# A two-layer hybrid encoder in float32: seven- and eight-product pairs alternate, weight sums one pair ahead, banks emptied by token tile, side loads on GpSimd's queue

## The chip, the core and the metric

The kernel runs on one core of a Trainium2 chip. Its engines are TensorE (PE, the matmuls; its weight loads are listed as PEld), VectorE (DVE), ScalarE (ACT), GpSimd (POOL) and SyncE (SP), which here does nothing but issue loads and stores. The metric is the device time of one execution in microseconds (us), the median of several runs.

## What is computed

An encoder with two layers over 256 tokens of width 2048, in float32. Each layer adds to x a mixer and then a feed-forward network (FFN):

```
h = rms_norm(x, g_mix[l])
z = h @ w_in[l]                          # one projection for mixer and memory queries
tok = chunked_spatial_gating(...)        # layer 0: gelu, 128-token chunks, 12 groups
tok = gqa_axial_attention(...)           # layer 1: 12 query heads, 4 key heads, QK norm, rotary
mem_out = memory_attention(q_mem, mem)   # both: 4 heads over 256 memory tokens
x = x + concat(tok, mem_out) @ w_out[l]
gate, up = split(rms_norm(x, g_ffn[l]) @ w_gate_up[l])   # 2048 -> 2 x 5632
x = x + (silu(gate) * up) @ w_down[l]                    # 5632 -> 2048
```

## The kernel before

**Tiles.** Tokens lie in two tiles (t = 0, 1) of 128. Weights are read in column blocks of 512 and rows (K blocks) of 128. Every product of float32 numbers is made of three matmuls of reduced operands, high x high, low x high and high x low (`matmul3`, L195 to L197). A weight tile `raw` is cut by `halves`: ACT casts it to `whi` (L248), DVE subtracts to get `wlo` (L249). Activations are cut in the same way by `split` (L189, L190). Transposes are matmuls against `ident` (L201 for most, L473 for the softmax weights).

**Linear layers.** `Linear` runs a column block for both token tiles: load of four K blocks (L262), `halves`, 24 matmuls. All projections use it, w_down too.

**Gate and up.** `Pair` works one column block f of 512 gate and 512 up columns (11 of them) over 16 K blocks, two at a time: eight feature pairs i. A pair of two K blocks, two token tiles and two column blocks is a 2 x 2 product of blocks. `eight` does it with eight `matmul3`. `seven` does it with seven, in Winograd's form of Strassen's scheme: it needs sums of weights (`T`, L342 to L344, on DVE, and a second `halves` of T) and sums of activations (`activation_sums`, once for each layer and pair). The seven products land in banks 1 to 7 of the accumulators, eight's in banks 2, 3, 4 and 8. Banks 1, 5, 6, 7 come from a pool of four with the tag `m`, which transposes and scores use too; 2, 3, 4, 8 from a pool of four with the tag `acc`. When the sevens are through, `inner` adds banks 1, 5, 6, 7 into four tiles `e` (L372 to L376); when the last pair is through, `outer` adds banks 2, 3, 4, 8 to these (L381 to L385). Silu and the product follow, and later the transposes of the result (`turn_a`).

**Which pairs.** Pairs 0, 1, 2 are sevens. In block f = 0 of a layer the order is 3, 4, 5, 6, 7, 0, 1, 2 (the activation sums are not ready at first), in all others 0, 1, 2, 3, ..., 7. Blocks f = 0 to 3, 4 to 7 and 8 to 10 are each followed by the part of the down-projection that uses them, which `Linear` runs over four column blocks, and DVE adds the result to X.

**Order.** The program is written stage by stage. Work that is to stand further back is put there by `later(delay, fn)`, which counts ticks; a tick is called after a group of products (half a pair, or half a unit of `Linear`). From the order written so, a scheduler makes a fixed row of instructions for each engine; each engine works through its row in order and waits for semaphores.

**Queues and buffers.** SP's queue issues every weight load, the loads of the memory tokens (L524), their transposed copies to DRAM for layer 1 (`memT`, L535) and back, and `w_spatial` (L590); ACT's queue issues `g_v` (L592) and the small constants. `raw`, `whi` and `wlo` have three buffers each, `T` two. A load waits on its queue until its buffer is free, and what is behind it on that queue waits too.

**Memory.** `Memory.prep` loads eight pieces of the memory tokens, one for each tick in layer 0 and one for every second in layer 1, and two ticks later transposes each.

**Attention.** `attend` gives each block of four query heads: transposes of q, scores (128x256 matmuls), reduce (L454), exponentials on ACT (L458), reciprocal, scaling (L463), transposes (L473), weighting. The ticks at which its parts run are a tuple of four delays.

Of the kernel before, what the change touches and what calls it, by code (L numbers as in the profile page):

```python
# [16 lines left out]
P = 128  # L17
D = 2048
S = 256
DEPTH = 2  # L20
# [31 lines left out]
def encoder(ctx: ExitStack, tc: tile.TileContext, x, mem, g_mix, g_ffn, w_in_a, g_v_a, w_spatial, b_spatial,  # L52
# [191 lines left out]
    def halves(raw, n):  # L244

        hi = wp.tile([P, KC4, NB], F32R, tag="whi", name=nm("whi"))[:, :n]
        lo = wp.tile([P, KC4, NB], F32R, tag="wlo", name=nm("wlo"))[:, :n]
        nc.scalar.copy(hi, raw)  # L248
        nc.vector.tensor_tensor(lo, raw, hi.bitcast(F32), ALU.subtract)  # L249
        return [(hi[:, c, :], lo[:, c, :]) for c in range(n)]  # L250

    class Linear:
# [12 lines left out]
        def run(self, units):  # L265
            for k0, n in units:
# [3 lines left out]
                parts = halves(raw[:, :n], n)  # L270
# [23 lines left out]
    def activation_sums(a):  # L294

        res = []
        for c in (0, 2):
            q = big(F32, [P, 4, P])
            nc.vector.tensor_tensor(q[:, 0], a[1][:, c], a[1][:, c + 1], ALU.subtract)
            nc.vector.tensor_tensor(q[:, 2], a[1][:, c], a[0][:, c], ALU.subtract)  # L300
            nc.vector.tensor_tensor(q[:, 1], a[0][:, c], q[:, 0], ALU.subtract)
            nc.vector.tensor_tensor(q[:, 3], a[0][:, c + 1], q[:, 1], ALU.subtract)
            hi, lo = split(q, [P, 4, P])
            res.append([(hi[:, i, :], lo[:, i, :]) for i in range(4)])
        return res

    class Pair:
# [3 lines left out]
        def __init__(self, parts, sums, w, na, nb, order, fast):  # L311
            self.parts, self.sums, self.w, self.na, self.nb = parts, sums, w, na, nb
            self.order, self.fast, self.bank, self.part = order, fast, {}, {}
            last = [i for i in order if i in fast][-1]
            rest = [i for i in order if i not in fast]
            for i in order:
                raw = self.fetch(i)
                (self.seven if i in fast else self.eight)(i, raw)
                if i == last:
                    self.inner()  # L320
            self.outer(bool(rest))
# [8 lines left out]
        def add(self, name, a, b, i):  # L330
# [3 lines left out]
            some = len([x for x in self.order if x in self.fast])  # L334
            many = len(self.order) - some
            of = {1: some, 5: some, 6: some, 7: some, 8: 2 * many}.get(name, some + 2 * many)
            self.part[name] += 1
            matmul3(self.bank[name], a, b, self.part[name] == 1, self.part[name] == of)

        def seven(self, i, raw):  # L340
            T = room["p"].tile([P, KC4, NB], F32, tag="T", name=nm("T"), bufs=2)
            nc.vector.tensor_tensor(T[:, 0:2], raw[:, 1:4:2], raw[:, 0:1].to_broadcast([P, 2, NB]), ALU.add)  # L342
            nc.vector.tensor_tensor(T[:, 2], T[:, 0], raw[:, 3], ALU.add)  # L343
            nc.vector.tensor_tensor(T[:, 3], T[:, 2], raw[:, 2], ALU.add)  # L344
# [8 lines left out]
            for some in (inner, outer):  # L353
                for name, a, b in some:
                    self.add(name, a, b, i)
                tick()

        def eight(self, i, raw):
            w01, w00, w10, w11 = halves(raw, 4)
            get, k0, k1 = self.parts.get, 2 * i, 2 * i + 1  # L360
            for t, names in ((0, (2, 3)), (1, (4, 8))):
                for name, pair in zip(names, ((w00, w10), (w01, w11))):
                    self.add(name, get(k0, t), pair[0], i)
                    self.add(name, get(k1, t), pair[1], i)
                tick()

        def inner(self):

            b = self.bank
            tmp = [room["p"].tile([P, NB], F32, tag=f"e{i}", name=nm("e"), bufs=1) for i in range(4)]  # L370
            e, v, f, y = tmp
# [5 lines left out]
            self.tmp = tmp  # L377

        def outer(self, rest):
            b, (e, v, f, y) = self.bank, self.tmp  # L380
            nc.vector.tensor_tensor(e, b[2], e, ALU.add)  # L381
            nc.vector.tensor_tensor(v, b[4], v, ALU.subtract)
            nc.vector.tensor_tensor(f, b[3], f, ALU.add)
            if rest:
                nc.vector.tensor_tensor(y, b[8], y, ALU.add)  # L385
            self.out = [[e, f], [v, y]]
# [127 lines left out]
    class Memory:  # L514
# [5 lines left out]
        def prep(self, delay, apart):  # L520
            def load(j, t):
                m = big()
                src = memT[t][j] if self.l else mem[0, t * P:(t + 1) * P, j * NB:(j + 1) * NB]
                nc.sync.dma_start(m, src)  # L524
                later(2, lambda: piece(m, j, t))

            def piece(m, j, t):
# [7 lines left out]
                nc.sync.dma_start(memT[t][j], raw)  # L535
# [23 lines left out]
    def add_residual(acc, j, norm, g, parts):  # L559
# [7 lines left out]
        for t in range(NT):  # L567
            nc.vector.tensor_tensor(X[t][j], acc[t], X[t][j], ALU.add)
            later(1 + t, lambda t=t: turn(t))

# [3 lines left out]
    for l in range(DEPTH):  # L574
# [4 lines left out]
        if l == 0:  # L579
# [28 lines left out]
            def gate(t, c):  # L608
# [4 lines left out]
                sb[t][c] = big()  # L613
# [40 lines left out]
            m.prep(1, 1)  # L654
# [24 lines left out]
        else:  # L679
# [11 lines left out]
            for c in range(3):  # L691
                acc = linear(hT, w, c * NB)
                attend(head_norm(acc, norm.r, ghead["q"], True), (7, 8, 10, 12), lambda: own["k"], lambda: own["v"],
# [15 lines left out]
        fast = [0, 1, 2]  # L709
        slow = [3, 4, 5, 6, 7]  # L710
        sums = {}

        def feature_sums(j):
            whole = []
            for t in range(NT):
                hi, lo = hF.whole[j, t]
                a = big(F32, [P, 4, P])
# [83 lines left out]
```

## Time and profile before

| | |
|---|---|
| three runs | 2088.92, 2092.15, 2092.33 us, median 2092.15 |
| the profiled execution | 2092.77 us |
| its span | 2090.8 us |
| mean granted TensorE clock | 0.991 |
| DMA packets, bytes | 204,696, 396.0 MB, mean 189 GB/s |

The span runs from the first to the last instruction in the trace; the remaining 2 us of the profiled execution lie around it. Times in the trace are counted from the start of the span. In the views of the profile, a row of a group or of a timeline names the line, the engine, the operation and the tiles, output <- inputs; in square brackets stands how long the engine had been idle before it and what ended that. A row of the windows gives for each engine the busy time and, in brackets, the number of instructions; then the share of full clock that TensorE was granted, the DMA engines' busy share and GB/s.

### The profile page before, as it was taken

The numbers are of one execution on the slowest core, as the hardware profiler recorded it, in microseconds if no ns is written. First come the engines' busy times: TensorE is split into PE (matmuls) and PEld (weight loads), VectorE is DVE, ScalarE is ACT, GpSimd is POOL, SyncE is SP. The second block draws the span as 40 slices with busy tenths as digits, with TensorE's granted clock in tenths as the row PEclk, the third lists the DMA queues.
The fourth block names the chain that finished last, engine by engine and source line by source line (L and its number), as shares of the span: only waits on it lengthen the run. The fifth ranks groups of instructions, "written<-read, shape, count | busy, mean of one in ns | idle before, by whom it ended". The sixth has DMA issues, their size and how long they took to land.

```text
span 2090.8 us, 23855 instructions
## 1 busy us (share of the span) xinstructions
PE 2052.3 (98%) x9346; PEld 1697.9 (81%) x9346; DVE 1485.8 (71%) x1502; ACT 1038.9 (50%) x1150; POOL 39.3 (2%) x50
## 2 busy tenths in 40 slices
PE   8799999899999999999999999998999999999999
PEld 6688888688888888888888878877888888888887
DVE  5466557987578875787567776688965889657964
ACT  7555444545344543445555654544543456434542
POOL 0010000000000000000000010000000000000000
PEclk9899999999999999999999999999999999999999
DMA  8655555465556555656556534545565655656564
GB/s 274 233 173 165 187 181 181 162 201 199 184 192 210 201 194 189 201 191 204 186 171 224 172 121 161 182 161 181 181 213 190 202 181 194 210 200 201 178 211 135
DMA packets 204696, 396.01 MB, mean 189 GB/s; under 512 B 9660, under 2 KB 12840, under 8 KB 204584
## 3 DMA queue, kind: packets, MB, share of 16 engines
q1 hardware_dynamic: 202432, 392.86, 56.2%
q10 hardware_dynamic: 2152, 1.63, 0.3%
q8 instruction: 73, 1.20, 0.2%
q14 instruction: 39, 0.32, 0.0%
HBM read 390.26 MB, written 4.19 MB: 189 GB/s over the span
## 4 chain that ended last, share of the span: by engine, by line
PE 92%; DVE 3%; issue 2%; DMA 2%; ACT 1%; SPq 0%; ACTq 0%; DVEq 0%
PE acc L195 27%; PE acc L196 27%; PE acc L197 27%; PE m L195 3%; PE m L196 3%; PE m L197 3%; PE m L201 2%; DVE wlo L249 1%; DMA a<-in_mem 1%; ACT whi L248 1%; PE m L473 0%; DVE T L342 0%; DMA gh_mq<-in_g_mq 0%; PE m L612 0%; DVE T L343 0%
## 5 line engine op out<-in xcount | busy, mean ns | idle before, releaser
L249 DVE TENSOR_TENSOR wlo<-raw,whi 128x2048 fp32r<-128x2048 f32 (+3 forms) x369 | 797.2, 2165 | 368.9 <-ACT whi L248 367.4
L248 ACT CAST whi<-raw 128x2048 fp32r<-128x2048 f32 (+3 forms) x369 | 666.5, 1812 | 646.0 <-PE acc L196 559.6
L195 PE MATMUL acc<-whi,h 128*128 128x512 f32 x1428 | 561.2, 394 | 10.1 <-DVE e L381 8.3
L196 PE MATMUL acc<-whi,h 128*128 128x512 f32 x1428 | 559.0, 392 | 0.0
L197 PE MATMUL acc<-wlo,h 128*128 128x512 f32 x1428 | 540.9, 392 | 0.0
L195 PE MATMUL acc<-whi,a 128*128 128x512 f32 x1154 | 451.5, 392 | 0.6 <-DVE a L404 0.6
L197 PE MATMUL acc<-wlo,a 128*128 128x512 f32 x1154 | 449.7, 391 | 0.0
L196 PE MATMUL acc<-whi,a 128*128 128x512 f32 x1154 | 449.5, 391 | 0.0
L195 PEld LDWEIGHTS acc<-whi,h 128*128 128x128 f32 x1428 | 270.0, 189 | 65.6 <-DVE e L381 9.1
L196 PEld LDWEIGHTS acc<-whi,h 128*128 128x128 f32 x1428 | 269.9, 189 | 55.2
L197 PEld LDWEIGHTS acc<-wlo,h 128*128 128x128 f32 x1428 | 268.7, 188 | 55.5 <-DVE wlo L249 0.4
L197 PEld LDWEIGHTS acc<-wlo,a 128*128 128x128 f32 x1154 | 217.1, 188 | 44.8
L195 PEld LDWEIGHTS acc<-whi,a 128*128 128x128 f32 x1154 | 217.2, 188 | 44.4 <-DVE a L404 0.8
L196 PEld LDWEIGHTS acc<-whi,a 128*128 128x128 f32 x1154 | 217.1, 188 | 44.0
L248 ACT CAST whi<-T 128x2048 fp32r<-128x2048 f32 x66 | 126.2, 1913 | 118.3 <-PE acc L196 110.6
L249 DVE TENSOR_TENSOR wlo<-T,whi 128x2048 fp32r<-128x2048 f32 x66 | 150.9, 2287 | 29.6 <-ACT whi L248 29.6
L342 DVE TENSOR_TENSOR T<-raw 128x1024 f32<-128x1024 f32 x66 | 80.4, 1218 | 18.7 <-DMA raw<-in_w_gate_up 18.7
L195 PE MATMUL m<-whi,a 128*128 128x512 f32 x198 | 80.0, 404 | 1.8 <-ACT whi L248 1.8
L196 PE MATMUL m<-whi,a 128*128 128x512 f32 x198 | 79.4, 401 | 0.0
L189 ACT CAST a<-m 128x512 fp32r<-128x512 f32 x80 | 46.3, 585 | 41.2 <-PE m L197 17.9
L190 DVE TENSOR_TENSOR a<-m,a 128x512 fp32r<-128x512 f32 x80 | 54.1, 684 | 17.0 <-ACT a L189 17.0
L197 PE MATMUL m<-wlo,a 128*128 128x512 f32 x198 | 55.9, 391 | 1.3 <-DVE wlo L249 1.3
(123 smaller groups left out, 1262.3 us busy)
## 6 DMA issues: line engine op xcount, KB each, us to landing
raw<-in_w_gate_up SPq DMA_DIRECT2D x352, 512.0 KB, 4.6
raw<-in_w_down SPq DMA_DIRECT2D x88, 1024.0 KB, 5.1
raw<-in_w_out SPq DMA_DIRECT2D x32, 1024.0 KB, 5.1
raw<-in_w_in_a SPq DMA_DIRECT2D x24, 1024.0 KB, 5.1
raw<-in_w_in_b SPq DMA_DIRECT2D x24, 1024.0 KB, 5.2
raw<-in_w_mem_kv SPq DMA_DIRECT2D x16, 1024.0 KB, 5.2
raw<-in_w_in_a SPq DMA_DIRECT2D x7, 512.0 KB, 5.8
x<-in_x SPq DMA_DIRECT2D x8, 256.0 KB, 4.7
```

What stands on the lines that cost most here:

```text
L189: nc.scalar.copy(hi, src)
L190: nc.vector.tensor_tensor(lo, src, hi.bitcast(F32), ALU.subtract)
L195: nc.tensor.matmul(out, lhsT=a[0], rhs=b[0], start=start, stop=False)
L196: nc.tensor.matmul(out, lhsT=a[1], rhs=b[0], start=False, stop=False)
L197: nc.tensor.matmul(out, lhsT=a[0], rhs=b[1], start=False, stop=stop)
L201: nc.tensor.transpose(dst[:, c * P:(c + 1) * P], src[:, c * P:(c + 1) * P], ident)
L248: nc.scalar.copy(hi, raw)
L249: nc.vector.tensor_tensor(lo, raw, hi.bitcast(F32), ALU.subtract)
L342: nc.vector.tensor_tensor(T[:, 0:2], raw[:, 1:4:2], raw[:, 0:1].to_broadcast([P, 2, NB]), ALU.add)
```

## The change

- **Order of the pairs.** In f > 0: 0, 3, 1, 4, 2, 5, 6, 7. In f = 0: 3, 4, 5, 0, 6, 1, 7, 2, with only pairs 0 and 1 as sevens. The activation sums of pairs 0, 1, 2 are made one at a time, at ticks 2, 4, 6.
- **One pair ahead.** `run` loads the next pair and makes its T before it works on the present one, also across the border of two blocks f (`follow`).
- **Banks.** `outer(t)` adds token tile t's two banks right behind that tile's products of the last pair.
- **Down-projection.** It uses `Pair` too, on two column blocks at a time, and adds straight into X. In the first two of the three groups of blocks one pair (i = 2 f + 1 of the first f) is a seven, at the fourth place of the order.
- **Splits.** `Linear` cuts a `raw` tile in two steps of two K blocks each.
- **Side loads.** Memory tokens, `memT`, `w_spatial` and `g_v` are loaded from GpSimd's queue; the `memT` writes go on ACT's. In layer 0 the pieces load at every second tick and are used three ticks later.
- **Small.** The gating result reuses v's tile; the delays of the query heads are 7, 8, 11, 13 instead of 7, 8, 10, 12.

The core of the diff:

```diff
-    def halves(raw, n):
+    def halves(raw, n, step=KC4):
...
-        nc.scalar.copy(hi, raw)
-        nc.vector.tensor_tensor(lo, raw, hi.bitcast(F32), ALU.subtract)
+        for c in range(0, n, step):
+            cut = slice(c, min(c + step, n))
+            nc.scalar.copy(hi[:, cut], raw[:, cut])
+            nc.vector.tensor_tensor(lo[:, cut], raw[:, cut], hi[:, cut].bitcast(F32), ALU.subtract)
...
-                parts = halves(raw[:, :n], n)
+                parts = halves(raw[:, :n], n, KC2)
...
+        def run(self, follow=None):
+
+            for n, i in enumerate(self.order):
+                self.prepare(i)
+                if n + 1 < len(self.order):
+                    self.prepare(self.order[n + 1])
+                elif follow:
+                    follow.prepare(follow.order[0])
+                (self.seven if i in self.fast else self.eight)(i, *self.ready.pop(i))
+                if i == self.inmost:
+                    self.inner()
+
+        def prepare(self, i):
+
+            if i in self.ready:
+                return
+            raw = self.fetch(i)
+            self.ready[i] = (raw,)
+            if i in self.fast:
+                T = room["p"].tile([P, KC4, NB], F32, tag="T", name=nm("T"), bufs=2)
+                nc.vector.tensor_tensor(T[:, 0:2], raw[:, 1:4:2], raw[:, 0:1].to_broadcast([P, 2, NB]), ALU.add)
+                nc.vector.tensor_tensor(T[:, 2], T[:, 0], raw[:, 3], ALU.add)
+                nc.vector.tensor_tensor(T[:, 3], T[:, 2], raw[:, 2], ALU.add)
+                self.ready[i] = raw, T
...
         def eight(self, i, raw):
+            done = i == self.order[-1]
...
+                if done:
+                    self.outer(t)
                 tick()
...
+        def outer(self, t):
+
+            o = self.out
+            for n, name in enumerate(((2, 3), (4, 8))[t]):
+                op = ALU.subtract if name == 4 and not self.into else ALU.add
+                nc.vector.tensor_tensor(o[t][n], self.bank[name], o[t][n], op)
...
-                nc.sync.dma_start(m, src)
-                later(2, lambda: piece(m, j, t))
+                nc.gpsimd.dma_start(m, src)
+                later(3, lambda: piece(m, j, t))
...
-                nc.sync.dma_start(memT[t][j], raw)
+                nc.scalar.dma_start(memT[t][j], raw)
...
-                nc.sync.dma_start(v4(a), w_spatial[0, 4 * i:4 * i + 4].rearrange("g t s -> t g s"))
+                nc.gpsimd.dma_start(v4(a), w_spatial[0, 4 * i:4 * i + 4].rearrange("g t s -> t g s"))
                 gv[i] = big()
-                nc.scalar.dma_start(gv[i], g_v_a[0, i * NB:(i + 1) * NB].partition_broadcast(P))
+                nc.gpsimd.dma_start(gv[i], g_v_a[0, i * NB:(i + 1) * NB].partition_broadcast(P))
...
-            m.prep(1, 1)
+            m.prep(1, 2)
...
+            quick = [2 * chunk[0] + 1] if chunk[-1] < 10 else []
...
-                order = slow + fast if f == 0 else fast + slow
-                g = Pair(hF, sums, w_gate_up[l], f * NB, DFF + f * NB, order, fast)
+                order = (0, 3, 1, 4, 2, 5, 6, 7) if f else (3, 4, 5, 0, 6, 1, 7, 2)
+                pairs[f] = Pair(hF, sums, w_gate_up[l], f * NB, DFF + f * NB, order, fast if f else fast[:2])
+            for f, g in pairs.items():
+                g.run(pairs.get(f + 1))
...
-                acc = linear(aT, w_down[l], j * NB, units, KC4 * len(chunk))
...
+                order = list(slow)
+                order[3:3] = quick
+                into = [[X[t][2 * jj + n] for n in range(2)] for t in range(NT)]
+                pairs.append(Pair(aT, aS, w_down[l], 2 * jj * NB, (2 * jj + 1) * NB, order, quick, into))
+            for jj, g in enumerate(pairs):
+                g.run(None if jj else pairs[1])
```

How the change moves instructions shows best at three places. A name's number is that of its buffer in the program; a line's number differs, since the code got longer (L249 is L251, L342 to L344 are L343 to L345, L373 to L376 are L393 to L396, L381 to L385 are L408, L473 is L495, L524 is L546).

First, DVE at the border of blocks f = 0 and f = 1 of layer 0, `m` and `acc` being banks, `e` the tiles that gather them. Before:

```order
L249 TENSOR_TENSOR wlo_3027<-raw_3019,whi_3026 128x1536
L343 TENSOR_TENSOR T_3022<-T_3022,raw_3019 128x512
L342 TENSOR_TENSOR T_3065<-raw_3062 128x1024
L373 TENSOR_TENSOR e_3001<-m_2921,e_3000 128x512
L344 TENSOR_TENSOR T_3022<-T_3022,raw_3019 128x512
L343 TENSOR_TENSOR T_3065<-T_3065,raw_3062 128x512
L374 TENSOR_TENSOR e_3002<-m_2913,e_3001 128x512
L381 TENSOR_TENSOR e_3000<-acc_2648,e_3000 128x512
L344 TENSOR_TENSOR T_3065<-T_3065,raw_3062 128x512
L375 TENSOR_TENSOR e_3001<-m_2917,e_3001 128x512
L376 TENSOR_TENSOR e_3003<-m_2917,e_3002 128x512
L249 TENSOR_TENSOR wlo_3031<-T_3022,whi_3030 128x2048
```

Now, at the same border:

```order
L393 TENSOR_TENSOR e_3022<-m_2947,e_3021 128x512
L251 TENSOR_TENSOR wlo_3110<-raw_3061,whi_3109 128x1536
L345 TENSOR_TENSOR T_3064<-T_3064,raw_3061 128x512
L394 TENSOR_TENSOR e_3023<-m_2939,e_3022 128x512
L395 TENSOR_TENSOR e_3022<-m_2943,e_3022 128x512
L396 TENSOR_TENSOR e_3024<-m_2943,e_3023 128x512
L408 TENSOR_TENSOR e_3021<-acc_2741,e_3021 128x512
L343 TENSOR_TENSOR T_3148<-raw_3145 128x1024
L251 TENSOR_TENSOR wlo_3114<-T_3064,whi_3113 128x2048
L408 TENSOR_TENSOR e_3023<-acc_2748,e_3023 128x512
L408 TENSOR_TENSOR e_3022<-acc_2771,e_3022 128x512
L408 TENSOR_TENSOR e_3024<-acc_2778,e_3024 128x512
```

Before, two T's (two sevens) are made among the bank sums, and the last T's split stands behind them; now each T stands by itself with the split of an eight between, and the four sums of `acc` stand ahead of and among the first splits of f = 1.

Second, the queues early in layer 0. SP's row before (`raw` are weights, `a` memory tokens, `memT` the copies for layer 1):

```order
L262 DMA raw_1071<-in_w_in_a 128x4x512
L524 DMA a_625<-in_mem 128x512
L535 DMA memT_1_110<-a_609 128x512
L262 DMA raw_1144<-in_w_mem_kv 128x4x512
L262 DMA raw_1174<-in_w_mem_kv 128x4x512
L524 DMA a_664<-in_mem 128x512
L535 DMA memT_1_114<-a_642 128x512
L524 DMA a_697<-in_mem 128x512
```

POOL's row now, where these loads stand:

```order
L546 DMA a_488<-in_mem 128x512
L546 DMA a_522<-in_mem 128x512
L546 DMA a_575<-in_mem 128x512
L546 DMA a_628<-in_mem 128x512
L546 DMA a_689<-in_mem 128x512
L616 DMA a_703<-in_w_spatial 128x4x128
L618 DMA a_705<-in_g_v_a 128x512
L546 DMA a_746<-in_mem 128x512
L616 DMA a_748<-in_w_spatial 128x4x128
L618 DMA a_750<-in_g_v_a 128x512
L616 DMA a_764<-in_w_spatial 128x4x128
L618 DMA a_766<-in_g_v_a 128x512
```

The loads of the memory tokens have left the row of weight loads and stand in one row with those of `w_spatial` and `g_v`, with no weight load between them.

Third, PE in the last block of query heads of layer 1 (128x256 matmuls are scores, `x4` four transposes of softmax weights). Before, from the end of the first two heads' scores on:

```order
L196 MATMUL m_8985<-a_7901,a_8953 128x256
L197 MATMUL m_8985<-a_7903,a_8951 128x256
L196 MATMUL m_9002<-a_7901,a_8953 128x256
L197 MATMUL m_9002<-a_7903,a_8951 128x256
L195 MATMUL m_9066<-a_7901,a_8952 128x256
L196 MATMUL m_9066<-a_7901,a_8954 128x256
L197 MATMUL m_9066<-a_7903,a_8952 128x256
```

Now, from the same point on:

```order
L196 MATMUL m_9288<-a_8155,a_9239 128x256
L197 MATMUL m_9288<-a_8157,a_9237 128x256
L195 MATMUL acc_9333<-whi_9558,a_8849 128x512
L196 MATMUL acc_9333<-whi_9558,a_8850 128x512
L197 MATMUL acc_9333<-wlo_9559,a_8849 128x512
L195 MATMUL m_9354<-a_8155,a_9238 128x256
L196 MATMUL m_9354<-a_8155,a_9240 128x256
L197 MATMUL m_9354<-a_8157,a_9238 128x256
```

Before, the scores of the last two heads (`m_9066`) follow at once, with the transposes right behind them; now three matmuls of the block that ends (`acc_9333`) stand between the scores of the first two heads (`m_9288`) and those of the last two (`m_9354`), and the transposes follow behind these.

More of the change, by code (lines that the diff above doesn't have):

```diff
@@ L285, in linear @@
         return Linear(parts, w, n0, nk).run(units)
[L294 to L305, printed above, removed]
@@ L307, in encoder, with activation_sums @@
-    class Pair:
[L311 to L319, printed above, removed]
-                    self.inner()
-            self.outer(bool(rest))
+    def activation_sums(a0, a1):
+        q = big(F32, [P, 4, P])
+        nc.vector.tensor_tensor(q[:, 0], a1[:, 0], a1[:, 1], ALU.subtract)
+        nc.vector.tensor_tensor(q[:, 2], a1[:, 0], a0[:, 0], ALU.subtract)
+        nc.vector.tensor_tensor(q[:, 1], a0[:, 0], q[:, 0], ALU.subtract)
+        nc.vector.tensor_tensor(q[:, 3], a0[:, 1], q[:, 1], ALU.subtract)
+        hi, lo = split(q, [P, 4, P])
+        return [(hi[:, i, :], lo[:, i, :]) for i in range(4)]
@@ new lines, in encoder, with __init__ @@
+    class Pair:
+        def __init__(self, parts, sums, w, na, nb, order, fast, into=None):
+            self.parts, self.sums, self.w, self.na, self.nb, self.into = parts, sums, w, na, nb, into
+            self.bank, self.part, self.ready = {}, {}, {}
+            self.order, self.fast = order, fast
+            some = [i for i in order if i in fast]
+            many = len(order) - len(some)
+            self.of = {1: len(some), 5: len(some), 6: len(some), 7: len(some), 8: 2 * many}
+            self.most = len(some) + 2 * many
+            self.inmost = some[-1] if some else None
+            self.out = into
+        def run(self, follow=None):
[7 more added lines that the diff above has]
+                if i == self.inmost:
+                    self.inner()
+        def prepare(self, i):
[9 more added lines that the diff above has]
+                self.ready[i] = raw, T
@@ L328, in fetch, with add @@
             return raw
-        def add(self, name, a, b, i):
+        def add(self, name, a, b):
             if name not in self.bank:
@@ L333, in add, with seven @@
                 self.part[name] = 0
-            some = len([x for x in self.order if x in self.fast])
-            many = len(self.order) - some
-            of = {1: some, 5: some, 6: some, 7: some, 8: 2 * many}.get(name, some + 2 * many)
             self.part[name] += 1
[L338 to L344, printed above, removed]
+            matmul3(self.bank[name], a, b, self.part[name] == 1, self.part[name] == self.of.get(name, self.most))
+        def seven(self, i, raw, T):
             W = halves(raw[:, 1:4], 3)
@@ L567, in add_residual, with residual_turns @@
         for t in range(NT):
-            nc.vector.tensor_tensor(X[t][j], acc[t], X[t][j], ALU.add)
+            if acc:
+                nc.vector.tensor_tensor(X[t][j], acc[t], X[t][j], ALU.add)
             later(1 + t, lambda t=t: turn(t))
+    def residual_turns(j, norm, g, parts):
+        add_residual(None, j, norm, g, parts)
     hT = Parts()
@@ new lines, in encoder @@
+                    later(3 + t if f == chunk[-1] else 12 + t, lambda a=a, t=t, f=f: turn_a(a, t, f))
+            last = chunk[-1] == 10
+            every = [2 * f + c for f in chunk for c in range(2)]
+            slow = [i for i in every if i not in quick]
+            pairs = []
+            for jj in range(2):
+                order = list(slow)
+                order[3:3] = quick
+                into = [[X[t][2 * jj + n] for n in range(2)] for t in range(NT)]
+                pairs.append(Pair(aT, aS, w_down[l], 2 * jj * NB, (2 * jj + 1) * NB, order, quick, into))
```

88 lines of the change are left out of this document (41 added, 47 removed).

## The prediction

> **What bounds the kernel now.** I read the page's head first, then the waits of TensorE (PE), then windows around each wait, then the instructions of PE inside them.
>
> ```profile
> span 2090.8 us, 23855 instructions
> ...
> PE 2052.3 (98%) x9346; PEld 1697.9 (81%) x9346; DVE 1485.8 (71%) x1502; ACT 1038.9 (50%) x1150; POOL 39.3 (2%) x50
> ...
> PE 92%; DVE 3%; issue 2%; DMA 2%; ACT 1%; SPq 0%; ACTq 0%; DVEq 0%
> ```
>
> The span, the busy times and the chain that ended last all say PE. But a busy PE is not PE at its pace, so the pace comes from starts near the end of the run, and that of transposes from a row of four:
>
> ```profile
> 82.86 0.60 PE L201 MATMUL m<-ident,a 128*128 128x128 f32 x4
> ...
> 2077.77 0.39 PE L195 MATMUL acc<-whi,a 128*128 128x512 f32 x1
> ...
> 2085.93 0.39 PE L195 MATMUL acc<-whi,a 128*128 128x512 f32 x1
> ```
>
> 36 intervals lie between these two starts: 8.16 / 36 = 0.2267 us for one 128x512 matmul. Everything above that pace is lost. The waits of PE (total, times, longest) say who is waited for:
>
> ```profile
> PE m L201 <- DMA a<-in_mem: 11.0, 2, 10.7
> ...
> PE acc L195 <- DVE e L381: 8.3, 2, 4.2
> ...
> PE m L197 <- DVE wlo L249: 3.5, 4, 1.1
> ...
> PE m L473 <- DVE a L463: 2.7, 1, 2.7
> ```
>
> The windows say where (length, PE busy, PEld busy, DVE busy, ACT busy, POOL busy, then granted clock, DMA share, GB/s):
>
> ```profile
> 0.00:40.00 40.00, 33.63 (x146) 25.77 (x147) 23.72 (x49) 29.37 (x64) 3.14 (x14) 1.00 0.85 276
> 80.00:100.00 20.00, 9.02 (x36) 6.95 (x35) 8.99 (x18) 11.74 (x29) 0.16 (x1) 0.66 0.70 228
> 380.00:408.00 28.00, 21.46 (x73) 15.45 (x72) 25.51 (x26) 17.42 (x13) 0.00 (x0) 0.82 0.36 114
> 408.00:1220.00 812.00, 812.00 (x3701) 674.11 (x3699) 599.79 (x597) 403.75 (x441) 16.70 (x14) 1.00 0.58 194
> 1220.00:1245.00 25.00, 21.74 (x118) 18.62 (x116) 18.03 (x38) 14.40 (x43) 2.53 (x2) 0.93 0.49 169
> 1408.00:1438.00 30.00, 22.64 (x77) 16.46 (x76) 27.54 (x27) 17.57 (x14) 0.00 (x0) 0.83 0.37 116
> ```
>
> From 408 to 1220 us PE never stops at full clock, through ten of the eleven column blocks f of layer 0's FFN, all three down-projections and the head of layer 1. Little is left to win there except matmuls. The loss stands in four places. **Memory tokens**, 80 to 100: 12 of the 36 records are transposes (0.15 us each, by the row at 82.86); 24 matmuls at pace are 5.4 us, so 12.8 to 14.6 are lost, I take 13.6. **FFN start of layer 0**, 380 to 408: 4 transposes, 69 matmuls are 15.6; 11.8 to 12.4 lost, I take 12.1. **FFN start of layer 1**, 1408 to 1438: 73 matmuls are 16.5; 12.9 to 13.5, I take 13.2. **Last query block of the attention**, 1220 to 1245; its matmuls are of mixed width, so I add up gaps (and show the first start of layer 0's FFN for its pace):
>
> ```profile
> 384.87 0.50 PE L195 MATMUL acc<-whi,h 128*128 128x512 f32 x1 [4.17 <-DVE e L381]
> ...
> 386.28 0.63 PE L195 MATMUL m<-whi,a 128*128 128x512 f32 x1
> ...
> 386.71 0.63 PE L196 MATMUL m<-whi,a 128*128 128x512 f32 x1
> ...
> 1237.75 0.63 PE L473 MATMUL m<-ident,a 128*128 128x128 f32 x4 [2.68 <-DVE a L463]
> ...
> 1238.95 0.54 PE L195 MATMUL acc<-whi,a 128*128 128x512 f32 x1 [0.58 <-DVE a L404]
> ...
> 1242.70 0.40 PE L195 MATMUL acc<-whi,a 128*128 128x512 f32 x1
> ```
>
> 2.68 + 0.58 us of waits, and from 1238.95 to 1242.70 nine matmuls at 0.42 instead of 0.23, 1.7 more; with the slow transposes 5.3. The half pace behind a gap is part of its price. Together 44.2 us. The Trainium skill, "TensorE: Matmul & The Clock Gate", section "What's actually happening", puts half clock behind an idle window of about 3.4 us. The trace agrees behind the 4.17 us wait for L381 (starts 0.43 apart at 386), but in the attention 2.68 us did it as well; by that rule a leftover attention gap would cost itself only, by the row about twice itself.
>
> **The change, part by part.**
>
> *Fewer products.* Counted from the code. Gate/up, per block f: 3 x 7 + 5 x 8 = 61 products as before, 62 at f = 0 (two sevens now): +1 for each layer, 3 matmuls each, +6. Down: one seven-product pair for each of 2 column halves, in two chunks, in two layers: 8 products saved, -24. Net -18 x 0.2267 = **-4.1 us**, safe as long as PE is the bound.
>
> *Memory loads.* Eight loads of `mem` (L524) stand on SP's queue between weight loads, each of which waits for a free `raw` buffer:
>
> ```profile
> 94.20 1.09 PE L201 MATMUL m<-ident,a 128*128 128x128 f32 x4 [10.75 <-DMA a<-in_mem]
> ...
> 37.70 15.23 SPq L262 DMA_DIRECT2D raw<-in_w_in_a  x5
> ...
> 81.70 6.35 SPq L262 DMA_DIRECT2D raw<-in_w_mem_kv  x2
> ...
> 88.10 0.50 SPq L524 DMA_DIRECT2D a<-in_mem  x1
> ...
> 89.12 0.62 SPq L524 DMA_DIRECT2D a<-in_mem  x1
> ...
> a<-in_mem SPq DMA_DIRECT2D x8, 256.0 KB, 6.6
> ```
>
> The last two were issued at 88 and 89 us, behind two memory-weight loads that sat 6.35 us on the queue for their buffers; PE stood 10.75 us. Now these eight loads and six side loads (w_spatial, g_v) stand in GpSimd's (POOL's) queue, with nothing of the weights among them, and each piece is used three ticks after its load instead of two, at every second tick. The next bound is the queue itself: first load at about 38 us, last transposes at PE's matmul 460, which at 146 matmuls by 40 us is 105 to 111 us. Fourteen loads in (105 - 38) us allow 4.8 us each if they went one after the other. The trace has no load from POOL; SP's need 0.5 to 0.6 us to issue and 6.6 to land, overlapping (two issued 1.0 us apart). At 0.6 each nothing is late; at 6.6 strictly in series the last would land at 38 + 92 = 130, 25 us late, so -13.6 becomes +11. I take the issue price, since the rows overlap, and leave 1 us: **-12.6**. The removed loads also let SP run ahead with weights; the memT writes now on ACT's queue cost 8 x 0.6 on an engine half idle.
>
> The Trainium skill speaks against this move: "SBUF — State Buffer", section "SBUF: two separate sides", says that descriptors of GpSimd's loads are written by GpSimd, which cannot while DVE holds the shared port, and gives some 3.1 us for such a load instead of 0.62. No run here shows it yet; at 3.1 us the fourteen would end at about 81 us, still ahead of PE.
>
> *Sevens and eights alternate.* What a pair costs DVE:
>
> ```profile
> L249 DVE TENSOR_TENSOR wlo<-raw,whi 128x2048 fp32r<-128x2048 f32 x294 | 671.7, 2290 | 362.6 <-ACT whi L248 362.1
> ...
> L342 DVE TENSOR_TENSOR T<-raw 128x1024 f32<-128x1024 f32 x66 | 80.4, 1218 | 18.7 <-DMA raw<-in_w_gate_up 18.7
> ...
> L343 DVE TENSOR_TENSOR T<-T,raw 128x512 f32<-128x512 f32 x66 | 45.4, 687 | 1.2
> ...
> L344 DVE TENSOR_TENSOR T<-T,raw 128x512 f32<-128x512 f32 x66 | 45.2, 686 | 0.6
> ...
> L249 DVE TENSOR_TENSOR wlo<-raw,whi 128x1536 fp32r<-128x1536 f32 x66 | 115.6, 1751 | 1.4 <-ACT whi L248 0.4
> ...
> L249 DVE TENSOR_TENSOR wlo<-T,whi 128x2048 fp32r<-128x2048 f32 x66 | 150.9, 2287 | 29.6 <-ACT whi L248 29.6
> ...
> 431.00:473.00 42.00, 42.00 (x191) 34.79 (x190) 37.41 (x32) 21.82 (x17) 0.00 (x0) 1.00 0.58 192
> ```
>
> A seven takes DVE 1.22 + 0.69 + 0.69 + 1.75 + 2.29 = 6.6 us against 21 x 0.2267 = 4.8 of PE; an eight 2.3 against 5.4. Three sevens in a row run up 5.6 us of debt, five eights pay it back. Where f = 0 ends with its three sevens and f = 1 begins with three, the debt is 11 us with no eight between: that is the 12 to 13 us at each FFN start, DVE busy 25.51 of 28 while PE waits for L249 and, behind it in DVE's row, for the bank sum L381. Now seven and eight alternate: 8.9 of DVE against 10.2 of PE, and f = 0 ends with an eight. A whole f stays as it is, 37.41 of 42 us of DVE, so 4.6 are free in each. Going through DVE's new row at these prices, the closest of the splits behind f = 0 comes 0.4 us ahead of PE. What is late next is such a split. Bounds: all cured (-25.3), or half left (-12.7) as three sevens' debt of the six might stay. I take 1 us left at each: **-23.3**.
>
> *Weight sums one pair ahead, next block's first included.* Same instructions, earlier: T's three sums (2.6 us) leave the way between load and split. They now wait for a load on a DVE that has splits queued behind them; L342's 18.7 us of idle before it in 66 is what that can bring, some 0.3 each. DVE has 4.6 free in each f.
>
> *Banks emptied by token tile.* Two sums (L381's kind, 0.7 us) move from behind the last product to behind its first half. From 408 to 1220 PE waits at no such boundary, so it can't gain; if the sums push a split back, each of 34 boundaries (11 f and 6 down halves in each layer) might stall. On the new rows the slack is 1.3 us or more, over half a `wlo`. **0**, bounds 0 to 14 (0.4 us each, the size of the closest slack).
>
> *Splits in halves* (Linear only): two casts and two subtracts for one, about 0.15 us more of DVE for each unit by 1.22 x 2 against 2.29, hidden beside a DVE with spare time:
>
> ```profile
> 518.00:606.00 88.00, 88.00 (x393) 72.87 (x393) 49.77 (x36) 31.88 (x19) 0.00 (x0) 1.00 0.57 191
> ```
>
> The down-projection leaves DVE 38 of 88 us free: its new seven-pair adds some 4.3 us of weight work and a few small sums for each half, which fits twice over. **0**.
>
> *Attention.*
>
> ```profile
> 1232.33 1.92 ACT L248 CAST whi<-raw 128x2048 fp32r<-128x2048 f32 x1
> ...
> 1233.43 0.69 DVE L454 TENSOR_REDUCE s<-m 128x2 f32<-128x512 f32 x1 [2.43 <-PE m L197]
> ...
> 1235.50 0.51 ACT L458 ACTIVATE a<-m,s 128x256 f32<-128x256 f32 x1
> ...
> 1237.26 0.61 DVE L463 TENSOR_SCALAR a<-a,s 128x256 f32<-128x256 f32 x2
> ```
>
> The half-wide cast no longer holds ACT for 1.92 us at once, and three block matmuls now stand between the heads' scores, so PE has 2.7 us of work where it had 2.2 against a softmax chain of about 3.1 (reduce 0.69, two exponentials at 0.51 partly overlapped, some 0.8, scale 0.61, and a second reduce and hand-overs of 1). 0.4 to 3 us may remain with its half pace; I take 2 of the 5.3: **-3.3**.
>
> *Sum*, against the profiled execution of 2092.77 us (span 2090.8): -4.1 - 12.6 - 23.3 - 3.3 = -43.3, which gives 2049.5. That execution lies 0.6 above the median of 2092.15, so on the scale of the median **2049 us**.
>
> **The rivals.**
>
> *Half of the FFN starts' wait stays.* DVE at f = 0 also carries the activation sums of three pairs, and 0.4 us of slack is thin. For: DVE is 89% busy in a steady f. Against: that f loses nothing. 12.7 left of 25.3 instead of 2, and half clock: 2060 to 2073.
>
> *Boundaries turn into waits.* PE queues the next seven behind `wlo` of a pair whose T was made ahead, and DVE does four bank sums in the same place. For: the co-limit of 89%. Against: slack counted at 1.3 us or more. 34 x up to 1 us: 2055 to 2083.
>
> *The memory loads come partly late from POOL*, in series near their landing time of 6.6 us: 13 to 25 us back, 2061 to 2075.
>
> *Slower than before.* The same mechanism at a higher price: the fourteen loads in series at more than (105 + 43 - 38) / 14 = 7.9 us each, over the 6.6 of a whole landing, would cost more than all else gains: 2097 and up. Only if POOL's queue neither overlaps loads nor keeps SP's pace.
>
> *It doesn't do what it says*: the T made ahead is held up by its own load (raw has three buffers), so sevens run as before, and only the memory loads and the products are won: 2092.8 - 4.1 - 12.6, about 2072 to 2078 with a little of the attention.
>
> **How the numbers follow.** Forecast (2042 to 2056) 0.70; half of the starts stays 0.10; boundaries 0.07; loads partly late 0.05; not as it says 0.04; slower 0.03; 0.01 for no change. Range 2042 to 2066: it leaves out the upper parts of the rivals. Faster by over 0.2% (4.2 us, about what a measurement of this kernel can tell from no change) 0.96, within it 0.01, slower 0.03.
>
> **What would show it.** In the changed profile: no wait of PE for in_mem, and POOL issuing the fourteen loads within 40 us of the first; PE at full clock through the FFN starts, with no wait for `e` there; DVE still near 89% in a steady f; at most a gap of 3 us ahead of the last query block's transposes; 18 matmuls fewer. It is wrong if half clock shows at 380 or 1400 us, or if small PE waits for `wlo` recur once for each f.

## The result, and the profile after

The changed kernel takes **2055.24 us** (median of four runs, 2053.78 to 2058.05) against 2090.53 us for the kernel before on the same chip: a ratio of 0.9833, 95% interval 0.9816 to 0.985. The forecast was 2049 in a range of 2042 to 2066. A later set of runs of the same kernel gave 2054.43. The profiled execution is the slowest of the first four, 2058.05 us, with a span of 2056.3; what follows is read from it.

The head of the page, to set beside the one of before:

```profile
span 2056.3 us, 24438 instructions
...
PE 2038.5 (99%) x9328; PEld 1688.9 (82%) x9328; DVE 1549.7 (75%) x1699; ACT 1061.5 (52%) x1270; POOL 47.5 (2%) x72
...
PE 97%; DMA 2%; DVE 1%; ACT 0%; issue 0%; ACTq 0%; SPq 0%; DVEq 0%
```

18 records of PE fewer, as counted, and a chain that is PE for 97% of the span in place of 92%. The waits of PE (total, times, longest) show what is gone and what is new:

```profile
PE acc L195 <- ACT whi L250: 5.2, 4, 2.7
PE m L132 <- DMA gst_mix<-in_g_mix: 4.3, 1, 4.3
PE acc L195 <- ACT h L222: 2.1, 1, 2.1
PE m L201 <- DMA x<-in_x: 0.9, 2, 0.4
PE acc L195 <- DVE a L426: 0.6, 1, 0.6
PE m L495 <- DVE a L485: 0.2, 1, 0.2
```

No wait for in_mem, none for `e`, and 0.2 us where the attention waited 2.7. The windows at the four old places and at the start (columns as before; the FFN and attention places come some 10 to 27 us earlier now):

```profile
20.00:60.00 40.00, 35.80 (x146) 27.18 (x145) 21.67 (x37) 25.90 (x48) 9.27 (x17) 0.91 0.90 303
80.00:100.00 20.00, 20.00 (x93) 16.56 (x92) 9.69 (x15) 15.48 (x32) 0.00 (x0) 1.00 0.65 203
370.00:400.00 30.00, 29.81 (x132) 24.33 (x131) 27.05 (x26) 15.32 (x11) 0.00 (x0) 1.00 0.64 214
1195.00:1225.00 30.00, 29.18 (x161) 24.93 (x160) 19.48 (x38) 16.06 (x44) 3.98 (x3) 1.00 0.43 145
1375.00:1408.00 33.00, 32.64 (x142) 26.00 (x141) 31.92 (x28) 17.50 (x13) 0.00 (x0) 1.00 0.49 162
```

The last four run at full clock. At 0.2267 us each, 132 records are 29.9 of 30 us and 142 are 32.2 of 33: the losses at the FFN starts have all but vanished. The first row is the bad news. The same 40 us of the kernel before:

```profile
20.00:60.00 40.00, 39.99 (x184) 31.95 (x183) 26.58 (x39) 29.63 (x53) 1.50 (x4) 1.00 0.85 297
```

184 matmuls then, 146 now: 34 fewer of 128x512 (161 to 127) and four transposes fewer (20 to 16), so 34 x 0.2267 + 4 x 0.15 = 8.3 us are lost in a stretch that lost nothing. Marks in the program say where the 34.5 us of span lie. These are summaries of one line each: durations (min/median/max in ns), then first and last start. The Gelu behind the first column blocks and the Silu behind each block f, before:

```profile
L663 ACT ACTIVATE a<-acc,s x6: 683/690/693, 39.4 to 112.7; 128x512 f32<-128x512 f32 x6
...
L676 ACT ACTIVATE a<-acc,s x6: 681/686/690, 200.0 to 248.4; 128x512 f32<-128x512 f32 x6
...
L743 ACT ACTIVATE sg<-e,s x44: 716/722/727, 387.7 to 2022.2; 128x512 f32<-128x512 f32 x44
```

and after:

```profile
L689 ACT ACTIVATE a<-acc,s x6: 681/690/696, 50.7 to 117.2; 128x512 f32<-128x512 f32 x6
...
L702 ACT ACTIVATE a<-acc,s x6: 678/688/690, 196.6 to 245.1; 128x512 f32<-128x512 f32 x6
...
L778 ACT ACTIVATE sg<-e,s x44: 713/718/727, 378.0 to 1987.4; 128x512 f32<-128x512 f32 x44
```

The first Gelu comes 11.3 us later (39.4 to 50.7), the first one behind the memory stage 3.4 earlier, the first Silu 9.7 earlier, the last 34.8 earlier. So the start gave away 11, and what was to be won was won: 14.7 between the first two marks alone.

### The profile page after: what moved, and what is told of

Its sections match the earlier page's. It is cut to its first block, busy times and chain, and to the rows that moved or that the text cites. A ratio compares the mean times of both kernels' runs of the same rounds, so it can differ in the third digit from the quotient of the medians.

```text
span 2056.3 us, 24438 instructions
## 1 busy us (share of the span) xinstructions
PE 2038.5 (99%) x9328; PEld 1688.9 (82%) x9328; DVE 1549.7 (75%) x1699; ACT 1061.5 (52%) x1270; POOL 47.5 (2%) x72
## 4 chain that ended last, share of the span: by engine, by line
PE 97%; DMA 2%; DVE 1%; ACT 0%; issue 0%; ACTq 0%; SPq 0%; DVEq 0%
PE acc L197 28%; PE acc L195 28%; PE acc L196 28%; PE m L197 4%; PE m L195 4%; PE m L196 3%; PE m L201 2%; DMA raw<-in_w_in_a 1%; PE m L495 0%; DMA gh_mq<-in_g_mq 0%; DVE wlo L251 0%; ACT whi L250 0%; DMA raw<-in_w_gate_up 0%; PE m L638 0%; DMA x<-in_x 0%
## 5 line engine op out<-in xcount | busy, mean ns | idle before, releaser
L251 DVE TENSOR_TENSOR wlo<-raw,whi 128x2048 fp32r<-128x2048 f32 (+3 forms) x465 | 800.5, 1742 | 303.1 <-ACT whi L250 302.1
L197 PE MATMUL acc<-wlo,h 128*128 128x512 f32 x1440 | 529.2, 394 | 0.1
L195 PE MATMUL acc<-whi,a 128*128 128x512 f32 x1112 | 435.8, 392 | 0.6 <-DVE a L426 0.6
L196 PE MATMUL acc<-whi,a 128*128 128x512 f32 x1112 | 433.9, 390 | 0.0
L197 PE MATMUL acc<-wlo,a 128*128 128x512 f32 x1112 | 426.0, 391 | 0.0
L197 PEld LDWEIGHTS acc<-wlo,a 128*128 128x128 f32 x1112 | 208.8, 188 | 43.1
L195 PEld LDWEIGHTS acc<-whi,a 128*128 128x128 f32 x1112 | 208.9, 188 | 42.8 <-DVE a L426 0.8
L196 PEld LDWEIGHTS acc<-whi,a 128*128 128x128 f32 x1112 | 209.0, 188 | 42.1
L250 ACT CAST whi<-T 128x2048 fp32r<-128x2048 f32 x72 | 137.8, 1913 | 145.1 <-DVE T L345 97.7
L251 DVE TENSOR_TENSOR wlo<-T,whi 128x2048 fp32r<-128x2048 f32 x72 | 164.8, 2290 | 29.9 <-ACT whi L250 26.0
L343 DVE TENSOR_TENSOR T<-raw 128x1024 f32<-128x1024 f32 x72 | 88.0, 1222 | 20.9 <-DMA raw<-in_w_gate_up 18.5
L196 PE MATMUL m<-whi,a 128*128 128x512 f32 x224 | 87.2, 389 | 0.0
L195 PE MATMUL m<-whi,a 128*128 128x512 f32 x224 | 87.2, 389 | 0.0
L408 DVE TENSOR_TENSOR e<-acc,e 128x512 f32<-128x512 f32 x88 | 59.2, 687 | 17.7 <-PE acc L197 17.1
L190 DVE TENSOR_TENSOR a<-m,a 128x512 fp32r<-128x512 f32 x80 | 54.3, 687 | 17.8 <-ACT a L189 17.7
```

Source lines behind the costliest of these rows:

```text
L190: nc.vector.tensor_tensor(lo, src, hi.bitcast(F32), ALU.subtract)
L195: nc.tensor.matmul(out, lhsT=a[0], rhs=b[0], start=start, stop=False)
L196: nc.tensor.matmul(out, lhsT=a[1], rhs=b[0], start=False, stop=False)
L197: nc.tensor.matmul(out, lhsT=a[0], rhs=b[1], start=False, stop=stop)
L250: nc.scalar.copy(hi[:, cut], raw[:, cut])
L251: nc.vector.tensor_tensor(lo[:, cut], raw[:, cut], hi[:, cut].bitcast(F32), ALU.subtract)
```

## The experiments

Expectations that speak of the first Gelu count its table load, which starts 1.3 us ahead of it (38.1 before, 49.4 in the changed kernel). What happens at the start shows in POOL's row of the changed kernel (start, duration, operation, count; in brackets idle time and what ended it):

```profile
24.91 2.90 POOL L546 DMA_DIRECT2D a<-in_mem  x5
27.81 0.77 POOL L616 DMA_DIRECT2D a<-in_w_spatial  x1
28.57 0.54 POOL L618 DMA_DIRECT2D a<-in_g_v_a  x1
29.10 0.54 POOL L546 DMA_DIRECT2D a<-in_mem  x1
29.63 0.76 POOL L616 DMA_DIRECT2D a<-in_w_spatial  x1
30.38 0.54 POOL L618 DMA_DIRECT2D a<-in_g_v_a  x1
31.07 0.75 POOL L616 DMA_DIRECT2D a<-in_w_spatial  x1 [0.16 <-issue]
```

Eleven loads of 256 KB in 6.9 us, one behind the other, with nothing of the weights that holds them back (the expectation of e1 counts twelve). Before, SP's row had the first three of the memory loads behind seven weight loads:

```profile
31.61 1.52 SPq L524 DMA_DIRECT2D a<-in_mem  x3
```

ACT's casts of the weights in that stretch of the changed kernel:

```profile
34.26 1.04 ACT L250 CAST whi<-raw 128x1024 fp32r<-128x1024 f32 x1 [5.18 <-DMA raw<-in_w_in_a]
...
44.04 2.00 ACT L250 CAST whi<-raw 128x1024 fp32r<-128x1024 f32 x2 [5.77 <-DMA raw<-in_w_in_a]
```

Two weight tiles are late by more than 5 us. ACT waits 13.3 us for w_in in the first 60 us, against 2.0 before, while the GB/s of the two windows above are nearly the same (303 and 297). What each queue moved in the first 60 us (packets, MB, share of the DMA engines' time; q1 is SP's queue, q0 GpSimd's), before:

```profile
q1 hardware_dynamic: 8287, 15.99, 79.1%
```

and after:

```profile
q1 hardware_dynamic: 6466, 12.52, 62.5%
q0 software_dynamic: 1040, 3.41, 18.5%
```

GpSimd's queue moved 3.41 MB and SP's 3.47 less than before; 1.3 of these are four loads of memory tokens and a memT write that have moved, some 2.1 are weights (by the sizes of the loads). The side loads took the weights' place. In the profile of the later set (e10, 2054.68 us) ACT waits 12.8 us for w_in, but the window from 20 to 60 us holds 159 matmuls, 21 of 128x512 and four transposes fewer than before, so the same burst costs 5.4 us there.

**Side loads back** (e1). `nc.gpsimd` to `nc.sync` for the memory tokens and w_spatial, to `nc.scalar` for g_v, the memT writes to `nc.sync`.

> The changed kernel with its side loads back on the queues they came from (memory tokens, memT writes and w_spatial on SP, g_v on ACT); the spacing of two ticks and the use three ticks later stay. Theory A (burst): in the changed kernel GpSimd issues twelve loads of 256 KB within 6.2 us, and these take the DMA engines from the w_in weights, so PE starves between 30 and 50 us. Then here the first Gelu comes near 38 us as before (49.4 in the changed kernel) and some 9 to 11 us are won at the start; the wait for in_mem near 80 to 100 us may come back, by 0 to 13 us. Time 2044 to 2058. Theory B: the late start has nothing to do with the side loads (the split casts, or the run). Then the first Gelu stays near 49 us and the time is 2055 to 2068.

2056.36 us (2055.37 to 2057.65). The first Gelu is back at 40.5 and ACT waits 3.5 us for w_in: theory A holds. But the total doesn't fall, since a wait comes later, from 108 to 113 us:

```profile
PE acc L195 <- ACT a L689: 5.7, 1, 5.7
```

Not the load but the Gelu behind it: ACT waits for in_mem (6.0 us between 80 and 116 us), works off the pieces, and the banks that PE needs are freed behind them. What the start wins is paid again there.

**Only the side loads, in the kernel before** (e2).

```diff
-                nc.sync.dma_start(m, src)
-                later(2, lambda: piece(m, j, t))
+                nc.gpsimd.dma_start(m, src)
+                later(3, lambda: piece(m, j, t))
...
```

The queues of w_spatial, g_v and the memT writes and the spacing of two ticks follow as in the change.

> The kernel before with the side loads alone moved to GpSimd's queue (memT writes to ACT's), two ticks apart and used three ticks later. Theory A (burst): the wait of 10.7 us for in_mem with its half clock goes (-13.6), and a new loss of 9 to 11 us between 30 and 50 us comes: 2085 to 2089, first Gelu near 49 us. Theory B: nothing is lost at the start: 2076 to 2078, first Gelu near 38 us.

2097.55 us against 2092.25, slower: ratio 1.0027 (1.0018 to 1.0036). Both theories missed. PE's waits:

```profile
PE acc L195 <- ACT a L663: 9.1, 1, 9.1
PE acc L195 <- DVE e L381: 8.3, 2, 4.2
PE acc L195 <- ACT whi L248: 6.5, 3, 4.7
```

The burst is there (ACT waits 13.0 us for w_in, first Gelu 48.9), the wait for in_mem is gone, and a new one of 9.1 us stands in its place, from 117 to 126 us. The move of the queue alone is worth less than nothing.

**Loads paced by the weights** (e3). A copy of one column on POOL ahead of each side load of layer 0:

```diff
+    def behind_weights(tile):
+        nc.gpsimd.tensor_copy(tile[:, :1], newest[0][:, 0, :1])
...
+                if not self.l:
+                    behind_weights(m)
                 nc.gpsimd.dma_start(m, src)
...
```

> The changed kernel with each side load of layer 0 held back on GpSimd's queue by a copy of one column of the weight tile that is fetched nearest to it, so that the load is issued when that weight has landed. Theory A (burst): the loads spread, w_in keeps its bandwidth, first Gelu at 38 to 42 us, no wait for in_mem; 2044 to 2049. Theory B: 2054 to 2057, first Gelu near 49 us.

2049.41 us (2047.75 to 2050.08), 0.4 above theory A's range, and the first Gelu with its table load at 40.4, where theory A had it. Its window, and a copy with the loads behind it in POOL's row:

```profile
20.00:60.00 40.00, 40.00 (x186) 32.25 (x185) 26.16 (x46) 28.81 (x58) 12.77 (x28) 1.00 0.87 304
```

```profile
38.31 0.91 POOL L257 COPY a<-raw 128x1 f32<-128x1 f32 x1 [2.44 <-DMA raw<-in_w_in_a]
39.16 1.31 POOL L554 DMA_DIRECT2D a<-in_mem  x2
```

186 matmuls in place of 146, at the same GB/s. In POOL's row the loads of in_mem lie between 39.2 and 69.6 us; PE waits for none of them.

**Old order of the pairs** (e4, then e6).

```diff
-                order = (0, 3, 1, 4, 2, 5, 6, 7) if f else (3, 4, 5, 0, 6, 1, 7, 2)
-                pairs[f] = Pair(hF, sums, w_gate_up[l], f * NB, DFF + f * NB, order, fast if f else fast[:2])
+                order = (0, 1, 2, 3, 4, 5, 6, 7) if f else (3, 4, 5, 6, 7, 0, 1, 2)
+                pairs[f] = Pair(hF, sums, w_gate_up[l], f * NB, DFF + f * NB, order, fast)
```

> The changed kernel with the old order of pairs in gate/up (f = 0: 3 4 5 6 7 0 1 2 with three sevens, f > 0: 0 to 7), the rest unchanged: two matmul products fewer than the changed kernel. Theory C (debt): the alternation is what cured the FFN starts; six sevens in a row put DVE some 11 us behind and each FFN start loses 10 to 13 us again: 2073 to 2081. Theory D: weight sums one pair ahead cured them; then the time stays within 3 us of the changed kernel, 2052 to 2058.

2067.70 us (2066.64 to 2068.74). This kernel leaves out the four sums of banks 2, 3, 4 and 8 in block f = 0 of each layer, so it flatters the old order a little. The next one has them, behind the last pair:

> The changed kernel with the old order of pairs in gate/up (f = 0: 3 4 5 6 7 0 1 2 with three sevens, the bank sums all behind the last pair there; f > 0: 0 to 7). Theory C (debt): each FFN start loses 7 to 12 us, since six sevens follow each other: 2068 to 2079. Theory D: the alternation is worth nothing once T is made ahead: 2052 to 2058.

2072.96 us (2070.66 to 2074.65), 17.7 more than the changed kernel: theory C. Windows of e6 at the two FFN starts:

```profile
374.00:402.00 28.00, 21.49 (x87) 15.42 (x88) 25.54 (x26) 17.67 (x14) 0.00 (x0) 1.00 0.42 138
1388.00:1418.00 30.00, 24.47 (x88) 17.69 (x87) 27.54 (x27) 17.44 (x14) 0.00 (x0) 0.89 0.40 133
```

DVE busy for 25.5 of 28 and 27.5 of 30 us, PE with 87 and 88 records where 123 and 132 would fit. Less the four transposes of each that is 28 - 83 x 0.2267 - 0.6 = 8.6 and 30 - 84 x 0.2267 - 0.6 = 10.4: 19 of the 25 that the starts lost before. The other 6 belong to another edit; which one was not tried. The clock differs too: in e6 PE's longest wait there is 2.5 us and the granted clock 1.00 and 0.89, in the kernel before 4.2 us (for the bank sum `e`) and 0.82 and 0.83.

**Splits whole again** (e5).

```diff
-                parts = halves(raw[:, :n], n, KC2)
+                parts = halves(raw[:, :n], n)
```

> The changed kernel with Linear's splits whole again (one cast and one subtract of 128x2048 in place of two of each of 128x1024). Theory E: the split in halves is what lets small work between: where ACT and DVE take turns on a memory piece, each turn then stands behind a subtract of 2.29 us instead of 1.14, the pieces back up on ACT, and PE waits for the Gelu behind them near 115 us by 5 to 12 us, as in the run of the kernel before with the side loads on GpSimd (9.1 us); in the last query block of the attention the gap of 2.7 us with its half pace returns too: 2060 to 2073. Rival: the halves only cost DVE time; the time stays or falls, 2052 to 2057.

2074.14 us (2072.80 to 2074.62): 18.9 more, 1 us above theory E's range. Two of PE's waits in e5:

```profile
PE acc L195 <- ACT a L689: 9.1, 1, 9.1
...
PE m L495 <- DVE a L485: 3.2, 1, 3.2
```

PE's waits in e5 add up to 24.8 us, against 13.3 in the changed kernel; the rest of the 18.9 goes with the granted clock, 0.994 over the span against 0.998. ACT's row of e5 as it works off the memory pieces:

```profile
110.54 0.37 ACT L222 ACTIVATE a<-m,gcol_mem 128x128 fp32r<-128x128 f32 x1 [2.36 <-DVE a L223]
...
122.31 0.37 ACT L222 ACTIVATE a<-m,gcol_mem 128x128 fp32r<-128x128 f32 x1 [2.35 <-DVE a L223]
...
127.69 0.69 ACT L689 ACTIVATE a<-acc,s 128x512 f32<-128x512 f32 x1
```

and of the changed kernel:

```profile
109.41 0.59 ACT L556 COPY a<-m 128x512 f32<-128x512 f32 x1 [1.48 <-DVE a L223]
...
115.34 0.37 ACT L222 ACTIVATE a<-m,gcol_mem 128x128 fp32r<-128x128 f32 x1 [1.48 <-DVE a L223]
...
116.61 0.70 ACT L689 ACTIVATE a<-acc,s 128x512 f32<-128x512 f32 x1
```

ACT and DVE take turns on a piece (L222, L223); each time DVE is in a subtract of a weight tile, ACT stands for it, 2.36 us behind a whole one, 1.48 behind a half (which takes 1.22 us, not the 1.14 of the expectation). From 51 to 128 us ACT waits 22.3 us for L223 in e5 and 12.9 in the changed kernel. The Gelu (L689), behind the pieces on ACT, comes 11 us later, and PE waits 9.1 us for it, as in e2. The attention's wait comes back too (3.2 us for the scaled softmax weights, before 2.7).

The edit moved more than itself in both places. With whole splits the scheduler puts the casts of eight weight tiles between the second and the third Gelu in ACT's row, in place of six; and in the last query block it puts the scores of the heads in one piece again, with no block matmuls ahead of the last two heads, as in the kernel before. So the length of the subtract and the new order weren't told apart.

**Not ahead; sums last** (e7, e8). e7 leaves out the calls of `prepare` for the next pair; e8 puts both `outer` calls behind the last product.

> The changed kernel with each pair loaded, and its T made, when its turn comes and not one pair ahead. Theory C (debt): with sevens and eights in turn DVE has 1.3 us to spare in each two pairs and nothing is lost in a steady block; at most 2 us for each FFN start and border: 2054 to 2062. Theory F: the three sums of T, 2.6 us, stand in the way of each seven and PE waits once or more for each block f: 22 blocks by 0.5 to 2 us: 2066 to 2100.

> The changed kernel with the sums of both token tiles behind the last pair's last product, not behind each tile's. The prediction's view: PE waits at no border, so the place of two sums is worth nothing: 2053 to 2058. Rival: four sums in a row on DVE (2.4 us) hold back the next split or the banks at each of 34 borders by 0.3 to 1 us: 2065 to 2089.

2054.74 us (2054.37 to 2057.73) and 2054.67 (2053.36 to 2055.83): no difference from 2055.24. The reason is simpler than either expectation: in the programs as built, the rows of all five engines are the same as the changed kernel's in both, operation by operation, buffer numbers apart. The scheduler had put the loads and the sums there already. So these two are further runs of the changed kernel; what a late T would cost was not measured.

**Both undone** (e9), **the changed kernel again** (e10), **paced, spread wider** (e11, `later(10 + 2 * i, ...)` for w_spatial and g_v).

> The changed kernel with both undone: side loads back on SP's and ACT's queues, and Linear's splits whole. With it the four kernels of queue (SP or GpSimd) by split (whole or halves) are complete: changed kernel 2055, halves with SP 2056, whole with GpSimd 2074. If the halves are worth the same whichever queue the loads stand on (theory G: what PE waits for near 100 us is the turn-taking of ACT and DVE on the memory pieces), this one loses some 15 to 19 us against the kernel with halves and SP: 2071 to 2075. If the halves only pay where the loads come from GpSimd (theory H: with SP the load itself is late, splits or not), it loses the attention's 4 us and little else: 2058 to 2064.

> The changed kernel itself, as the measure beside the next run: 2053 to 2058, first Gelu 47 to 50 us.

> The paced kernel (each side load of layer 0 behind a copy of one column of the weight tile nearest to it) with the loads of w_spatial and g_v two ticks apart instead of one, so that no more than three side loads are let go by one weight tile. If what is left of the burst still costs weights their time (ACT waits 4.9 us for w_in in the paced kernel, 2.0 in the kernel before), 1 to 3 us less than it: 2046 to 2049. If nothing is left of it, 2048 to 2051. Either way faster than the changed kernel beside it by 4 to 9 us.

e9: 2065.86 us (2063.85 to 2066.14), between the two theories; both missed. PE's waits in it:

```profile
PE m L201 <- DMA a<-in_mem: 9.6, 1, 9.6
...
PE m L495 <- DVE a L485: 3.2, 1, 3.2
```

The load of in_mem itself is late again: in SP's row the last one stands two memory-weight loads further back than in e1 and is issued at 112.3 us, against 100.4. e10: 2054.43. e11: 2048.52 (2047.63 to 2050.27), faster than e10 beside it by 5.9 us, and with a ratio to the kernel before of 0.9794 (0.978 to 0.9807) against e10's 0.9824 (0.981 to 0.9837). e3 and e11 can't be told apart, so whether the wider spread is worth anything stays open; both beat the changed kernel.

The four kernels of queue by split, all else as changed (us):

| | whole splits | splits in halves |
|---|---|---|
| side loads on SP and ACT | 2065.9 | 2056.4 |
| on GpSimd, let go at once | 2074.1 | 2055.2 |
| on GpSimd, paced by weights | not tried | 2049.4, 2048.5 |

## Why the prediction held, and where it didn't

**Right in the total for partly wrong reasons, and with luck.** With whole splits the kernel takes 2074.1 us (e5), outside the range of 2042 to 2066: that the forecast held rests on an edit that it priced at 0. Its own steps, one by one.

- *Fewer products*, -4.1: the profile shows 18 records fewer.
- *Alternation*, -23.3: the starts' 25.3 us fell to about 1 (the window at 370 has nothing left, that at 1375 has 0.8). Debt was the reason: the old order alone brings 19 us of it back (e6). The 0.4 us of slack that the closest split had was enough.
- *Memory loads*, -12.6: **this is the step that failed.** It asked only whether POOL's queue would be too slow ("The next bound is the queue itself") and took the loads to begin at about 38 us, though SP's row before has three of them at 31.6. They begin at 24.9 and go out at 0.54 to 0.77 each; the queue was too fast. On SP they had stood behind weight loads, and this order was at the same time the wait for in_mem and the weights' right of way. No term and no rival had that. Its price is the start: the first Gelu 11.3 us late, so that behind the memory stage the kernel is 3.4 us ahead where 12.6 were forecast. Pacing wins back some 5 to 7 in the total (e3, e11).
- The slow side of the same step didn't come. The issues took 0.54 to 0.77 us, and no wait for DVE shows in POOL's row. The Trainium skill ("SBUF — State Buffer", "SBUF: two separate sides") says which operations of DVE keep GpSimd from writing its descriptors meanwhile, a float32 copy from SBUF to SBUF among them. From 24 to 37 us DVE's row holds the two-input operations L251 and L223 and one small copy out of a bank, so no such copy stood in the way here.
- *Splits in halves*, 0: **the second error.** The working looked only at DVE's extra time, which is hidden, and, the attention apart, not at who stands in line behind a 2.29 us subtract. The edit is worth 9.5 us with the loads on SP and 18.9 with them on GpSimd (the table). On GpSimd it shortens the turns on the memory pieces (e5's rows of ACT), along with a new order of ACT's row; on SP it goes with an earlier load of in_mem (e1 against e9); the attention's wait goes with it on both. Without it the move to GpSimd costs 8 us (2065.9 to 2074.1; +5.3 in the kernel before, e2), with it the move brings 1. So the prediction credited the queue with what only the two edits together did.
- *Attention*, -3.3: 0.8 us of waits are left, less than the 2 taken. With whole splits 3.2 us return (e5, e9), and the scores stand as before there; whether the shorter casts and subtracts cure it or the matmuls between the scores, which came with them, wasn't told apart.
- *Weight sums ahead* and *banks by token tile*, 0 each: right, and for a plainer reason than slack, since the scheduler had them there anyway (e7, e8).
- *The signs*: all came but two. The fourteenth side load goes out at 69.8 us, 45 behind the first and not within 40; the other thirteen take 12 us. And DVE is busy for 38.97 of 42 us in a steady f (410 to 452 us), 93% and not near 89.

The rivals *half of the FFN starts' wait stays* and *boundaries* (up to 34 waits) are refuted by the windows at full clock, *memory loads partly late* and *slower, loads in series* by POOL's row and the missing wait for in_mem. *It doesn't do what it says* asked for 2072 to 2078, and this didn't come; what a T held up by its own load would cost stays open (e7).

The total is 6 us above the forecast, and pacing the loads takes off as much: 2048.5 to 2049.4. The memory loads fell short by more, some 9 us (3.4 for 12.6); the alternation and the attention, which brought some 2 more than taken, make up part of it.

## What to carry to other kernels

A queue that is shared is also an order: before loads are moved to an idle queue, ask what will then hold them back, and what they will displace; here one copied column of the tile they should follow was enough to pace them. A long instruction on an engine that others take turns with can be a cost to the turn-takers, though the engine has time to spare. And where a scheduler sets the rows, see whether an edit changes them before pricing it.

## What the runs showed of the hardware

At the start of the changed kernel's run two waits of PE of only 2.07 and 2.13 us were each followed by a stretch at half clock. The windows, and the rows with the start and the idle time in brackets:

```profile
30.00:40.00 10.00, 7.93 (x26) 5.28 (x26) 3.91 (x13) 2.82 (x7) 2.74 (x5) 0.83 1.02 330
40.00:50.00 10.00, 7.87 (x26) 5.63 (x26) 3.88 (x5) 4.57 (x5) 0.00 (x0) 0.83 0.89 314
```

```profile
35.62 1.31 PE L195 MATMUL acc<-whi,h 128*128 128x512 f32 x2 [2.07 <-ACT h L222]
...
45.14 0.51 PE L195 MATMUL acc<-whi,h 128*128 128x512 f32 x1 [2.13 <-ACT whi L250]
...
46.99 0.63 PE L195 MATMUL acc<-whi,h 128*128 128x512 f32 x1
...
47.42 0.63 PE L196 MATMUL acc<-whi,h 128*128 128x512 f32 x1
```

A granted clock of 0.83 over 10 us is some 3.4 us at half clock in each window (an estimate from the two rows). The second wait comes behind matmuls at full pace (0.23 us apart), and behind it four more start at that pace or near it before the starts are 0.43 apart. Both waits are shorter than the 2.68 us of the attention before, and than the idle window of about 3.4 us that the Trainium skill names ("TensorE: Matmul & The Clock Gate", "What's actually happening"). In the profile of e10 a wait of 1.65 us, with one of 0.24 just behind it, did it as well, and one of 0.95 did not. The least wait that does it is not known from this.

Loads issued by GpSimd landed like SP's: 7.7 us for a memory piece in the first 60 us, 7.8 from SP before.
